# Low parts of streamed weights: VectorE's subtraction, or ScalarE's negation and an accumulating DMA

## The chip, the cores and the metric

The kernel runs on one core of a Trainium2 chip. Its engines work side by side, each on its own queue, in order, and wait for one another by semaphores: TensorE (PE; its weight loads are PEld), VectorE (DVE), ScalarE (ACT), GpSimd (POOL) and SyncE (SP, which here only starts DMAs). Sixteen DMA engines move data for all queues. The metric is device microseconds of one execution; a time is the median of several runs.

## The reference

Two decoder layers on 512 tokens of width 1024, all in float32. Layer 0 mixes tokens by gated linear attention (GLA), layer 1 by a gated DeltaNet in chunks; after each comes a ConvFFN of inner width 2816, and after every part a LayerNorm of the scaled residual:

```python
for i in range(DEPTH):                       # 2
    y = gla_mixer(h, ...) if i % 3 == 0 else gdn_mixer(h, ...)
    h = layer_norm(ALPHA * h + y, ln_g[i, 0], ln_b[i, 0])
    h = layer_norm(ALPHA * h + conv_ffn(h, ffn_w_in[i], ffn_conv_w[i], ffn_w_out[i]),
                   ln_g[i, 1], ln_b[i, 1])

def conv_ffn(x, w_in, conv_w, w_out):
    h = causal_dwconv(x @ w_in, conv_w)
    gate, up = jnp.split(h, 2, axis=-1)
    return (gelu(gate) * up) @ w_out
```

Most of the work is x @ w with large weights. The DeltaNet also solves a lower triangular system in each chunk, from which the small matmuls called V and R below come.

## The kernel before

**Three products for one.** A float32 matrix product is made from parts in the rounded type float32r: a = ah + al, w = wh + wl, and a w is taken as ah wh + ah wl + al wh. So for each weight block a high part (wh, the block rounded) and a low part (wl, the block minus wh) must be formed on the chip.

**A block's way.** All weights are streamed once, in the order of a plan (`plan_fm`, `plan_tm`, `plan_out`, `plan_pad`, `plan_rep`), in blocks of 128 x 1024 floats, 512 KB. `issue` (line 202) handles one: SP starts the load into a tile `raw` (three buffers, `RAWB`), ScalarE casts it to `wh` (line 243), VectorE subtracts to get `wl` (line 244). `wh` and `wl` have four buffers each (`WB`). In an "fm" block the eight pieces of 128 x 128 are held still in the PE array and the 512 columns of x stream past: 8 x 3 = 24 matmuls, `fm_mms`, line 286. In a "tm" block the activations are held still and two rows of 512 weight columns stream past for four token blocks: 2 x 4 x 3 = 24 matmuls as well, `tm_half`, line 342. All matmuls are issued in `mm`, line 155.

**The last blocks of a sublayer** (`TAIL` = 4) lie in ordinary activation slots (`wsh`, `wsl`, lines 233 and 234, in two halves), so that the token blocks can be finished one after another and the four large buffers already hold the next sublayer's first blocks. A sublayer that follows a LayerNorm begins with four blocks on the first half of the tokens, then the same four on the second half (`HEADSTART`), since the second half of x comes later. Each block's buffer is given back only after its second half.

**How far ahead.** `weight()` hands out the next block and calls `prefetch`, which issues blocks up to `look` ahead of those taken, as long as fewer than four large buffers are held. `look` is `LOOKAHEAD`, 2, and larger at a tail. This sets the order in which the program is written; the framework's scheduler then orders each engine's queue by its own estimate of when things are ready, except PE, whose order mostly follows the generator tasks. Those are spawned by the code and paced by an estimated PE clock (`clk`, `pump`), and `vec` adds VectorE's estimated work to it.

**What else uses POOL and SP.** Residual tiles are scaled and shifted on POOL after a LayerNorm (lines 583 and 584, sixteen operations in each of two sublayers). The DeltaNet's residual goes to DRAM and back by POOL's queue (lines 576, 606, 609). In the DeltaNet, `base` (line 1068) runs a forward substitution of 31 steps on VectorE for all chunks at once (lines 1078 and 1080), copies the result (line 1083), stores it (SP, lines 1084 and 1085) and loads it back in pieces T and rm (SP and POOL, lines 1097 and 1100); `inverse` (line 1108) builds the chunk inverses from them by the matmuls V and R.

Of the kernel before, what the change touches and what calls it, by code (L numbers as in the profile page):

```python
# [8 lines left out]
F32 = mybir.dt.float32  # L9
# [4 lines left out]
ALU = mybir.AluOpType  # L14
# [3 lines left out]
S = 512  # L18
# [13 lines left out]
SLOTS = 53  # L32
RAWB = 3
WB = 4
LOOKAHEAD = 2
TAIL = 4
HEADSTART = 4
INV_DELAY = 18.0
# [10 lines left out]
def blk(i, n=P):  # L49
    return slice(i * n, i * n + n)  # L50


class Trunk:
# [148 lines left out]
    def issue(self, item):  # L202

        nc = self.nc
        if item[0] == "rep":
            return self.issue_rep(*item[1:])
        used = 1024
        raw = self.raw if self.issued == 0 else self.rp.tile([P, 1024], F32, name=self.uid("raw"), tag="raw")
        if self.issued == 0:
            pass  # L210
        elif item[0] == "fm":
            _, w, col = item
            nc.sync.dma_start(
                raw.rearrange("p (c f) -> p c f", c=NC),
                w[:, col:col + P].rearrange("(c p) f -> p c f", p=P))
        elif item[0] == "tm":
            _, w, row, n, col, _ = item
            used = n * S
            nc.sync.dma_start(
                raw[:, :used].rearrange("p (j f) -> p j f", j=n),  # L220
                w[row:row + n * P, col:col + S].rearrange("(j p) f -> p j f", p=P))
        else:
            nc.gpsimd.memset(raw, 0.0)
            r3 = raw.rearrange("p (c f) -> p c f", c=NC)
            for w, col, n, at in item[1]:
                nc.sync.dma_start(
                    r3[:, :, at:at + n],
                    w[:, col:col + n].rearrange("(c p) f -> p c f", p=P))
        if self.in_slots(item):
            w = []  # L230
            for j in range(used // S):
                wh, wl = self.slot("wsh", F32R), self.slot("wsl", F32R)
                nc.scalar.copy(wh, raw[:, blk(j, S)])
                nc.vector.tensor_sub(wl, raw[:, blk(j, S)], wh)
                self.vec(0.7)
                w.append((wh, wl))
            return w
        self.held += 1
        wh = self.wp.tile([P, 1024], F32R, name=self.uid("wh"), tag="wh")
        wl = self.wp.tile([P, 1024], F32R, name=self.uid("wl"), tag="wl")  # L240
        for n in (S, used) if self.issued == 0 else (used,):
            cols = slice(0 if n < used or self.issued else S, n)
            nc.scalar.copy(wh[:, cols], raw[:, cols])  # L243
            nc.vector.tensor_sub(wl[:, cols], raw[:, cols], wh[:, cols])  # L244
        self.vec(1.24)
        return [(wh[:, blk(j, S)], wl[:, blk(j, S)]) for j in range(used // S)]

    def issue_rep(self, w, col):

        nc = self.nc  # L250
        raw = self.rp.tile([P, 1024], F32, name=self.uid("raw"), tag="raw")
        r3 = raw[:, :P].rearrange("p (c f) -> p c f", c=NC)
        nc.sync.dma_start(r3, w[:, col:col + 16].rearrange("(c p) f -> p c f", p=P))
        self.held += 1
        wt = self.wp.tile([P, 1024], F32R, name=self.uid("wh"), tag="wh").rearrange("p (c f) -> p c f", c=NC)
        w5 = wt[:, :, :96].rearrange("p c (r t f) -> p c r t f", r=3, t=2)
        src = r3.unsqueeze(2).to_broadcast([P, NC, 3, 16])
        nc.scalar.copy(w5[:, :, :, 0, :], src)
        nc.vector.tensor_sub(w5[:, :, :, 1, :], src, w5[:, :, :, 0, :])
        return wt  # L260
# [109 lines left out]
    def out_proj(self, a, n, first, final):  # L370
# [3 lines left out]
        for hf in range(2):  # L374
# [20 lines left out]
            self.tm_half(a, n, TAIL if last else 1, done, last)  # L395
        self.look = LOOKAHEAD

# [60 lines left out]
    def load_x(self, x):  # L458
# [34 lines left out]
        def second():  # L493
            for tb in range(2, NTB):
                self.after = self.x_parts(tb)
                yield 1.2
            self.look = LOOKAHEAD

# [869 lines left out]
```

## Time and profile before

| | us |
|---|---|
| median of 3 runs | 1295.02 |
| lowest, highest run | 1292.35, 1297.74 |
| span of the profiled execution | 1300.2 |
| TensorE, VectorE, ScalarE, GpSimd busy in it | 1279.0, 790.2, 546.8, 111.0 |

The profile is of one execution. Of it only the span, from the first to the last instruction, is known; it lies 5.2 us above the median of the timed runs. Matmuls overlap in their pipeline, so the busy time of PE hides short gaps, and the mean of one matmul (370 to 390 ns) is longer than the time from one to the next; that is read from the chain, as a stretch divided by its matmuls. Idle time of an engine is put down to what ended it, in square brackets.

### The profile page before, as it was taken

The numbers are of one execution on the slowest core, as the hardware profiler recorded it, in microseconds if no ns is written. First come the engines' busy times: TensorE is split into PE (matmuls) and PEld (weight loads), VectorE is DVE, ScalarE is ACT, GpSimd is POOL, SyncE is SP. The second block draws the span as 40 slices with busy tenths as digits, with TensorE's granted clock in tenths as the row PEclk, the third lists the DMA queues.
The fourth block names the chain that finished last, engine by engine and source line by source line (L and its number), as shares of the span: only waits on it lengthen the run. The fifth ranks groups of instructions, "written<-read, shape, count | busy, mean of one in ns | idle before, by whom it ended". The sixth has DMA issues, their size and how long they took to land.

```text
span 1300.2 us, 17238 instructions
## 1 busy us (share of the span) xinstructions
PE 1279.0 (98%) x6666; PEld 1078.1 (83%) x6666; DVE 790.2 (61%) x1442; ACT 546.8 (42%) x1030; POOL 111.0 (9%) x150
## 2 busy tenths in 40 slices
PE   8999999999999999999999999999999999999996
PEld 6878888988888888889788889988888888888885
DVE  3673366676643466655799835669677653366656
ACT  3554443634421344425865535543554431244420
POOL 4000000070000000001111310100034000000000
PEclk9999999999999999999999968999999999999999
DMA  6421224143333333251543420333143333333331
GB/s 181 117 81 49 77 86 130 33 130 114 98 97 97 97 97 98 87 143 66 135 117 106 127 49 17 115 98 113 49 137 107 97 98 98 97 97 97 97 98 65
DMA packets 167089, 126.52 MB, mean 97 GB/s; under 512 B 16088, under 2 KB 139546, under 8 KB 167008
## 3 DMA queue, kind: packets, MB, share of 16 engines
q1 hardware_dynamic: 161728, 115.10, 30.0%
q0 software_dynamic: 3888, 8.50, 2.1%
q10 hardware_dynamic: 1392, 1.84, 0.4%
q8 instruction: 52, 0.85, 0.3%
q14 instruction: 29, 0.24, 0.1%
HBM read 119.63 MB, written 5.78 MB: 96 GB/s over the span
## 4 chain that ended last, share of the span: by engine, by line
PE 86%; issue 6%; DVE 5%; DMA 1%; ACT 1%; POOL 1%; DVEq 0%; POOLq 0%; ACTq 0%
PE fm L155 45%; PE tm L155 32%; PE o L155 1%; PE V L155 1%; PE R L155 1%; PE xT L166 1%; PE vn L155 1%; DVE ln_st L386 1%; PE pg L155 1%; PE yT L166 1%; PE qkT L166 1%; PE pq L155 0%; DMA gla_nw<-in_gla_norm_w_dram 0%; DVE wl L244 0%; DVE conv L940 0%
## 5 line engine op out<-in xcount | busy, mean ns | idle before, releaser
L244 DVE TENSOR_TENSOR wl<-raw,wh 128x1024 fp32r<-128x1024 f32 (+1 forms) x190 | 238.3, 1255 | 321.1 <-ACT wh L243 319.3
L155 PE MATMUL fm<-xh,wh 128*128 128x512 f32 (+1 forms) x1104 | 408.3, 370 | 0.4 <-ACT wh L243 0.4
L155 PE MATMUL fm<-xl,wh 128*128 128x512 f32 (+1 forms) x1104 | 404.8, 367 | 0.0
L155 PE MATMUL fm<-xh,wl 128*128 128x512 f32 (+1 forms) x1096 | 401.2, 367 | 2.5 <-DVE wl L244 2.5
L243 ACT CAST wh<-raw 128x1024 fp32r<-128x1024 f32 (+1 forms) x190 | 198.8, 1047 | 269.9 <-PE tm L155 159.4
L155 PEld LDWEIGHTS fm<-xh,wl 128*128 128x128 f32 x1096 | 207.4, 190 | 36.5 <-DVE wl L244 3.1
L155 PEld LDWEIGHTS fm<-xh,wh 128*128 128x128 f32 x1104 | 209.1, 189 | 34.2 <-ACT wh L243 1.2
L155 PEld LDWEIGHTS fm<-xl,wh 128*128 128x128 f32 x1104 | 209.3, 190 | 32.7
L643 DVE SCALAR_TENSOR_TENSOR conv<-fm,ffn_cw,conv 128x511 f32<-128x511 f32 (+1 forms) x176 | 130.7, 745 | 3.0
L155 PE MATMUL tm<-wl,gh 128*128 128x512 f32 x288 | 112.0, 389 | 0.0
L155 PE MATMUL tm<-wh,gh 128*128 128x512 f32 x288 | 112.0, 389 | 0.0
L155 PE MATMUL tm<-wh,gl 128*128 128x512 f32 x288 | 112.0, 389 | 0.0
L155 PE MATMUL tm<-wh,xh 128*128 128x512 f32 x192 | 79.5, 414 | 1.0 <-ACT qk L756 1.0
L417 ACT CAST gh<-conv 128x512 fp32r<-128x512 f32 x44 | 27.3, 621 | 124.7 <-DVE conv L658 124.6
L155 PE MATMUL tm<-wh,xl 128*128 128x512 f32 x192 | 75.4, 393 | 0.0
L155 PE MATMUL tm<-wl,xh 128*128 128x512 f32 x192 | 75.1, 391 | 0.0
L653 ACT ACTIVATE conv<-conv 128x512 f32<-128x512 f32 x44 | 27.8, 633 | 95.0 <-DVE conv L643 95.0
L155 PEld LDWEIGHTS tm<-wh,gh 128*128 128x128 f32 x288 | 54.1, 188 | 11.2
L155 PEld LDWEIGHTS tm<-wh,gl 128*128 128x128 f32 x288 | 54.1, 188 | 11.2
L155 PEld LDWEIGHTS tm<-wl,gh 128*128 128x128 f32 x288 | 54.1, 188 | 11.2
L641 ACT ACTIVATE conv<-fm,ffn_cw 128x512 f32<-128x512 f32 x88 | 59.9, 681 | 0.2
L940 DVE SCALAR_TENSOR_TENSOR conv<-fm,gdn_cw,conv 128x509 f32<-128x509 f32 (+2 forms) x72 | 53.2, 742 | 4.6 <-ACT conv L938 4.1
(274 smaller groups left out, 1555.4 us busy)
## 6 DMA issues: line engine op xcount, KB each, us to landing
raw<-in_ffn_w_in_dram SPq DMA_DIRECT2D x88, 512.0 KB, 3.7
raw<-in_ffn_w_out_dram SPq DMA_DIRECT2D x44, 512.0 KB, 3.7
raw<-in_gdn_w_in_dram SPq DMA_DIRECT2D x32, 512.0 KB, 4.0
raw<-in_gla_w_in_dram SPq DMA_DIRECT2D x23, 512.0 KB, 3.5
raw<-in_gla_w_out_dram SPq DMA_DIRECT2D x8, 512.0 KB, 3.5
raw<-in_gdn_w_out_dram SPq DMA_DIRECT2D x8, 512.0 KB, 3.8
hd<-h POOLq DMA_DIRECT2D x8, 256.0 KB, 2.5
dt<-drow POOLq DMA_DIRECT2D x8, 256.0 KB, 5.6
```

The costliest lines, as they stand in the source:

```text
L155: t = self.nc.tensor.matmul(out, a, b, start=start, stop=stop)
L166: t = self.nc.tensor.transpose(out, a, self.ident[:n, :n])
L243: nc.scalar.copy(wh[:, cols], raw[:, cols])
L244: nc.vector.tensor_sub(wl[:, cols], raw[:, cols], wh[:, cols])
L386: nc.vector.bn_stats(self.st[tb][:, hf, :], h)
L417: cast = self.nc.scalar.copy(dst_h, src)
L641: nc.scalar.activation(a, ps, AF.Identity, scale=tap(2))
L643: nc.vector.scalar_tensor_tensor(a[:, d:], ps[:, :S - d], tap(2 - d), a[:, d:], ALU.mult, ALU.add)
L653: nc.scalar.activation(a, a, AF.Gelu)
L940: self.conv = nc.vector.scalar_tensor_tensor(a[:, d:], ps[:, :S - d], tap(3 - d), a[:, d:], ALU.mult, ALU.add)
```

## The change

Two things change in how a low part is made, and one in how far ahead.

- From the seventh block of the plan on, and for all blocks in slots, VectorE's subtraction is gone. ScalarE writes the negated rounded block into `wl` (it reads the raw block, multiplies by -1 and rounds as it writes), and a DMA issued from POOL adds the raw block onto it, as float32: raw - round(raw). The raw tile is free only when this DMA has landed.
- The first six blocks (`DIRECT`) are made as before; one of them is the small block of `issue_rep`, which isn't changed.
- `LOOKAHEAD` is 3.

`vec` is no longer called for the low parts, so the estimate of VectorE's load that paces some tasks is smaller.

```diff
-LOOKAHEAD = 2
+LOOKAHEAD = 3
+DIRECT = 6
...
                 nc.scalar.copy(wh, raw[:, blk(j, S)])
-                nc.vector.tensor_sub(wl, raw[:, blk(j, S)], wh)
-                self.vec(0.7)
+                self.low(wl, raw[:, blk(j, S)])
...
+        if self.issued >= DIRECT:
+            nc.scalar.copy(wh[:, :used], raw[:, :used])
+            self.low(wl[:, :used], raw[:, :used])
+            return [(wh[:, blk(j, S)], wl[:, blk(j, S)]) for j in range(used // S)]
...
+    def low(self, wl, raw):
+
+        self.nc.scalar.mul(wl, raw, -1.0)
+        self.nc.gpsimd.dma_start(wl.bitcast(F32), raw, accum_op=ALU.add)
```

The new function makes every line behind it stand 9 lower. How the queues are ordered now is shown at three places.

On POOL, in the first feed-forward layer, the residual's operations (h times and plus gb) stood in one piece behind loads of constants (rows). Before:

```order
L439 DMA rows_847<-in_ffn_conv_w_dram 44x128
L439 DMA rows_849<-in_gdn_conv_w_dram 96x128
L583 TENSOR_TENSOR h_95<-h_95,gb_2425 128x512
L583 TENSOR_TENSOR h_97<-h_97,gb_2425 128x512
L583 TENSOR_TENSOR h_96<-h_96,gb_2427 128x512
```

Now, with the accumulating DMAs (wl from raw; wl_2530 is the low part of the layer's block 11, wl_2573 of block 12):

```order
L592 TENSOR_TENSOR h_97<-h_97,gb_2494 128x512
L255 DMA wl_2530<-raw_2527 128x1024
L593 TENSOR_TENSOR h_95<-h_95,gb_2498 128x512
L592 TENSOR_TENSOR h_96<-h_96,gb_2496 128x512
L593 TENSOR_TENSOR h_97<-h_97,gb_2498 128x512
L593 TENSOR_TENSOR h_96<-h_96,gb_2500 128x512
L592 TENSOR_TENSOR h_98<-h_98,gb_2496 128x512
L592 TENSOR_TENSOR h_99<-h_99,gb_2494 128x512
L593 TENSOR_TENSOR h_98<-h_98,gb_2500 128x512
L593 TENSOR_TENSOR h_99<-h_99,gb_2498 128x512
L592 TENSOR_TENSOR h_100<-h_100,gb_2496 128x512
L592 TENSOR_TENSOR h_101<-h_101,gb_2494 128x512
```

One more operation of this kind follows, and then the DMA for wl_2573: eleven stand between the two. Three more stand ahead of block 13's. The second feed-forward layer has the same pattern.

On VectorE, at the end of the DeltaNet's substitution (tt and tmp are its steps, dt the decay matrices multiplied by PE's products pq, conv the short convolutions). Before, from the first product with pq on:

```order
L1054 TENSOR_TENSOR dt_5226<-dt_5226,pq_6114 128x512
L1080 TENSOR_TENSOR tt_4778<-tt_4778,tmp_5769 128x9x23
L1078 TENSOR_TENSOR tmp_5769<-m_798_4779,tt_4778 128x192
L1080 TENSOR_TENSOR tt_4778<-tt_4778,tmp_5769 128x8x24
L1078 TENSOR_TENSOR tmp_5769<-m_798_4779,tt_4778 128x175
L1080 TENSOR_TENSOR tt_4778<-tt_4778,tmp_5769 128x7x25
L244 TENSOR_TENSOR wl_6235<-raw_6232,wh_6234 128x1024
```

Seventeen more rows stand between these and the copy of line 1083. Now:

```order
L1063 TENSOR_TENSOR dt_5344<-dt_5344,pq_6244 128x512
L1089 TENSOR_TENSOR tt_4883<-tt_4883,tmp_5893 128x2x30
L1087 TENSOR_TENSOR tmp_5893<-m_798_4884,tt_4883 128x31
L1089 TENSOR_TENSOR tt_4883<-tt_4883,tmp_5893 128x31
L1092 COPY m_798_4884<-tt_4883 128x1024
```

The first product with pq comes at the same place among PE's matmuls; on VectorE the substitution is all but finished there.

On PE, where the inverse begins. Before, after the eighteen matmuls of a block that follow the third pq (the last two are shown):

```order
L155 MATMUL fm_6238<-xl,wh_6085 128x512
L155 MATMUL fm_6238<-xh,wl_6086 128x512
L155 MATMUL V_6285<-T_6060,am_5522 32x32 x4
L155 MATMUL V_6285<-T_6060,am_5558 32x32 x4
L155 MATMUL V_6286<-T_6060,am_5522 32x32 x4
L155 MATMUL V_6286<-T_6060,am_5558 32x32 x4
L155 MATMUL R_6311<-V_6284,rm_6062 32x32 x4
```

Now, after six matmuls of that block:

```order
L156 MATMUL fm_6370<-xl,wh_6139 128x512
L156 MATMUL fm_6370<-xh,wl_6140 128x512
L156 MATMUL V_6417<-T_6189,am_5644 32x32 x4
L156 MATMUL V_6417<-T_6189,am_5680 32x32 x4
L156 MATMUL V_6418<-T_6189,am_5644 32x32 x4
L156 MATMUL V_6418<-T_6189,am_5680 32x32 x4
L156 MATMUL fm_6370<-xh,wh_6139 128x512
```

The first V is asked for twelve matmuls earlier, and nine large matmuls now stand between V and R. On SP a load of a raw tile stands just ahead of the first load of T, before and now; it waited for a subtraction and now waits for an accumulating DMA.

## The prediction

> **What bounds the kernel now.** I read the page's head first, then the chain of work that ended last, the list of what TensorE (PE) waited for, and the windows by stage.
>
> ```profile
> span 1300.2 us, 17238 instructions
> PE 1279.0 (98%) x6666; PEld 1078.1 (83%) x6666; DVE 790.2 (61%) x1442; ACT 546.8 (42%) x1030; POOL 111.0 (9%) x150
> L244 DVE TENSOR_TENSOR wl<-raw,wh 128x1024 fp32r<-128x1024 f32 (+1 forms) x190 | 238.3, 1255 | 321.1 <-ACT wh L243 319.3
> L243 ACT CAST wh<-raw 128x1024 fp32r<-128x1024 f32 (+1 forms) x190 | 198.8, 1047 | 269.9 <-PE tm L155 159.4
> ```
>
> The work to be replaced is VectorE's largest group, but VectorE is busy 61% and PE 98%. In the chain the two feed-forward layers are unbroken matmuls:
>
> ```profile
> 367.94 65.28 PE tm L155 x288
> 433.22 108.80 PE fm L155 x480
> ```
>
> Both rows give 0.227 us a matmul. Every weight block of 512 KB feeds 24 matmuls of 512 columns, so PE takes a block every 24 x 0.227 = 5.44 us, in both row kinds. Nothing that VectorE gives up can shorten that. What it can shorten is the list of PE's waits (the five longest of those that hang on weights, VectorE or the inverse):
>
> ```profile
> PE fm L155 <- DVE wl L244: 2.5, 3, 1.3
> PE V L155 <- DMA T<-dinvt: 1.1, 2, 0.6
> PE qkT L166 <- ACT conv L942: 1.1, 2, 0.7
> PE R L155 <- DMA rm<-dinv: 0.6, 1, 0.6
> PE xT L166 <- DVE ln_rs L538: 0.6, 1, 0.6
> ```
>
> and one stretch in which TensorE's clock was not granted in full. The columns of a window are its length, then busy time by engine, granted clock, DMA share and GB/s:
>
> ```profile
> 640.00:740.00 100.00, 98.80 (x509) 82.77 (x509) 91.76 (x245) 60.59 (x145) 19.66 (x39) 1.00 0.42 121
> 740.00:800.00 60.00, 58.26 (x609) 49.96 (x608) 24.00 (x53) 21.92 (x69) 11.19 (x20) 0.74 0.20 45
> 1270.00:1300.20 30.20, 19.90 (x88) 16.15 (x86) 22.08 (x60) 0.00 (x0) 0.00 (x0) 0.92 0.19 69
> 745.00:750.00 5.00, 4.40 (x53) 4.00 (x48) 1.53 (x6) 1.93 (x9) 4.83 (x9) 0.57 0.40 67
> ```
>
> In 640 to 740 VectorE is full (91.76 of 100): it runs the DeltaNet's forward substitution among the subtractions. Then the clock falls: 60 x (1 - 0.74) = 15.6 us of full-speed work are lost. The last 10 us (30.20 - 19.90) are the final LayerNorm, which has no weights in it.
>
> **The change part by part.**
>
> *VectorE loses* 184 subtractions of 128x1024 and 32 of 128x512 (the first five whole blocks stay): 184 x 1.255 + 32 x 0.68 = 253 us, of 790.
>
> ```profile
> L233 ACT CAST wsh<-raw x32: 609/620/632, 193.2 to 1252.9; 128x512 fp32r<-128x512 f32 x32
> L234 DVE TENSOR_TENSOR wsl<-raw,wsh x32: 675/683/693, 193.9 to 1253.6; 128x512 fp32r<-128x512 f32 x32
> ```
>
> *ScalarE gains* as many multiplications by -1. The trace has none of that shape; the cast beside it reads and writes the same sizes, so 184 x 1.05 + 32 x 0.62 = 213 us, making 760 of 1300 us. It stays below PE in every window (the fullest hundred, 640 to 740, goes from 61 to about 61 + 18 x 1.05 = 80).
>
> *What VectorE's room is worth.* In the substitution it sits in the way like this:
>
> ```profile
> 727.01 0.68 DVE L1054 TENSOR_TENSOR dt<-dt,pq 128x512 f32<-128x512 f32 x1
> 736.47 1.09 DVE L1083 COPY m<-tt 128x1024 f32<-128x1024 f32 x1
> 737.47 1.22 DVE L244 TENSOR_TENSOR wl<-raw,wh 128x1024 fp32r<-128x1024 f32 x1
> ```
>
> ```profile
> 742.89 0.66 PE L155 MATMUL V<-T,am 32*32 32x32 f32 x16 [0.65 <-DMA T<-dinvt]
> 746.29 0.63 PE L155 MATMUL R<-rm,V 32*32 32x32 f32 x8 [0.60 <-DMA rm<-dinv]
> ```
>
> Before, the copy that ends the substitution comes 9.5 us after the first product with pq; in the new order only three short steps lie between them, so the copy ends about 727.0 + 0.7 + 0.6 + 1.1 = 729.4, some 8 us earlier. PE asks for T twelve matmuls (2.7 us) earlier, so some 5 us remain for the two stores, the queue and the loads: the waits on T and rm go. What is late next there is SP, on which a raw load that waits for an accumulating DMA now stands ahead of the loads of T. Of the five waits above, 5.9 us in all, I count 5 us as gone (bounds 0 and 5.9).
>
> *The clock.* Whether it falls again is not settled by the trace. Less waiting and a more even mix with large matmuls speak for a shallower dip, the same tiny 32x32 matmuls against. Bounds 0 and -15.6; I take half, -7.8, because the fall begins in the very window that holds the two waits.
>
> *The DMA engines* get 184 accumulations of 512 KB and 32 of 256 KB. Neither their length nor their load is in the trace; the nearest rows are plain copies:
>
> ```profile
> q1 hardware_dynamic: 161728, 115.10, 30.0%
> raw<-in_ffn_w_in_dram SPq DMA_DIRECT2D x88, 512.0 KB, 3.7
> dinvt<-tt SPq DMA_DIRECT2D x1, 512.0 KB, 2.7
> 650.00:655.00 5.00, 5.00 (x23) 4.11 (x23) 3.78 (x8) 2.74 (x11) 0.00 (x0) 1.00 1.02 356
> ```
>
> Queue q1: 0.300 x 1300.2 = 390 us of all sixteen engines for 115.1 MB, 1.78 us a block. The fullest window moves 356 GB/s, 1.47 us a block. An accumulation reads two blocks and writes one, so one pass (1.5) to three (5.3) bound it; I take two full passes, 2.9 us, since a plain copy also reads and writes in one pass. With the load that is 4.7 of the 5.44 us: it fits, with little room. The Trainium skill's page "Collectives: The Full Stack", section "The bandwidth ceiling: the fold count and why AG ≠ RS ≠ AR", says the add itself costs nothing and the second read halves the rate (62.28 against 32.35 GB/s); by it an estimate is 1.93 x 1.47 = 2.8 us, and the sum would stay; no row here shows an accumulation. For the time from issue to landing I take the 2.7 us of the plain 512 KB copy plus one pass, 4.2 to 4.5: 4.4 us (bounds 2.7 and three times that, 8.1).
>
> *Is that hidden?* In a feed-forward layer ScalarE starts a block when PE frees the buffer of the block four back:
>
> ```profile
> 443.91 1.05 ACT L243 CAST wh<-raw 128x1024 fp32r<-128x1024 f32 x1 [0.96 <-PE fm L155]
> 444.86 0.68 ACT L641 ACTIVATE conv<-fm,ffn_cw 128x512 f32<-128x512 f32 x1
> ```
>
> Cast, conv and negation take 2.8 us, the issue on POOL 0.54 (row below), the landing 4.4: 7.7 us, against three blocks, 16.3 us. The raw tile is held 7.7 us and reloaded in 3.7 plus 0.4 of issue: 11.8 of the same 16.3 us for three raw tiles. Hidden at up to 12.2 us for the two landings together. Cost 0; this cover, three blocks of PE work, is also what "three ahead" keeps in program order.
>
> ```profile
> L576 POOL DMA_DIRECT2D hd<-h x8: 539/540/604, 584.5 to 605.2; - x8
> 614.40 1.05 ACT L243 CAST wh<-raw 128x1024 fp32r<-128x1024 f32 x1 [4.72 <-PE fm L155]
> 617.23 1.05 ACT L243 CAST wh<-raw 128x1024 fp32r<-128x1024 f32 x1 [1.20 <-PE fm L155]
> ```
>
> *At the start of a layer* the cover is thinner: four blocks are held until their second halves are done, 2.83 us apart. The fifth block is cast at 614.40, negated by 616.5, issued by 617.0, landed by 621.4; PE wants it at 614.40 + 3 x 2.83 + 0.45 = 623.3. Cost 0, at 8.1 us of landing 1.8 us, in three layers.
>
> *POOL's queue* is in order, and now carries the weights:
>
> ```profile
> 269.34 6.03 POOL L583 TENSOR_TENSOR h<-h,gb 128x512 f32<-128x512 f32 x4 [180.96 <-DMA gb<-in_ln_g_dram]
> L583 POOL TENSOR_TENSOR h<-h,gb x16: 1284/1514/2279, 269.3 to 983.6; 128x512 f32<-128x512 f32 x16
> 250.39 1.05 ACT L243 CAST wh<-raw 128x1024 fp32r<-128x1024 f32 x1 [6.35 <-PE fm L155]
> 253.27 1.05 ACT L243 CAST wh<-raw 128x1024 fp32r<-128x1024 f32 x1 [1.24 <-PE fm L155]
> ```
>
> The new order puts eleven of its residual operations between two accumulations. Block 5 of the layer starts at 250.39 + 3 x 2.88 = 259.0 and block 12 at 259.0 + 7 x 5.44 = 297.1. Block 11 is ready for issue at 275.3 + 2.8 = 278.1; eleven operations of 1.51 us end at 295.2; block 12 is issued by 295.8 and lands at 300.2, but its low part is wanted at 297.1 + 0.45: PE waits 2.7 us. It happens in both feed-forward layers: +5.4 us. Bounds: 0.2 us each with the shortest operations (1.284), 6.4 with a landing of 8.1.
>
> *The sum:* -5 - 7.8 + 5.4 = -7.4 us. The profiled execution (span 1300.2) lies 5.2 above the timed median of 1295.0, so I apply the difference to the median: **1287.6 us**. Its bounds without the extremes together: 1275 to 1302.
>
> **The rivals.**
>
> *1. The clock dip stays and the rest cancels.* For it: the tiny matmuls are all still there. The Trainium skill's page "TensorE: Matmul & The Clock Gate", section "What's actually happening", has half clock follow an idle window of about 3.4 us; by it the 0.65 us waits would not be its cause. The trace disagrees in part, as the clock fell to 0.57 with no longer wait. Time: -5 + 5.4, 1295.
>
> *2. The DMA engines become the bound.* With the load at 1.78 us, PE is overtaken once an accumulation takes over 5.44 - 1.78 = 3.7 us of all engines. Three passes at the fastest rate are 4.4 us: 6.2 us a block, 0.75 x 184 = 138 us slower, about 1425; at q1's rate 1600. For it: no row shows an accumulation; against it: two passes fit.
>
> *3. Landings are hidden in the mean but not at the seams.* At 8.1 us the two residual places cost 6.4 each and the three layer starts 1.8 each, 18 us, and a window like that of 745 to 750 loses 2 us of clock; with the 5 us won and the dip in place, about 1295 + 18 + 2 x 2 - 5 = 1312. It decides from a landing of about 6 us. For it: POOL's waits and residual work stand ahead of weights; against it: the plain copy's 2.7 us.
>
> **How the numbers follow.** The forecast has 0.50, rival 1 0.17, rival 2 0.18, rival 3 0.15. About 0.5% (6.5 us) is what a measurement of this kernel can tell from no change: faster means below 1288.5. Of the forecast's own range (1275 to 1302) seven tenths lie there, and a fifth of rival 1: 0.35 + 0.03 = 0.38. Slower: rivals 2 and 3 and a little of the forecast, 0.35. Same: 0.27. The range 1274 to 1335 takes in the forecast, rivals 1 and 3 and the mildest of rival 2, and leaves out most of rival 2.
>
> **What would show it.** Right: VectorE near 537 us, ScalarE near 760; in 370 to 540 PE still at 0.227 us a matmul with no waits; landings of 4 to 5 us; a DMA share near 0.8; the granted clock of the inverse's stretch well above 0.74; short waits on wl where POOL does the residual. Wrong: matmuls in the feed-forward layers spaced by waits on wl or wh (rival 2); a dip as deep as before (rival 1); waits on wl at all five seams (rival 3).

## The result, and the profile after

The changed kernel takes **1353.54 us** (median of 4 runs, 1346.74 to 1354.32) against 1296.38 for the kernel before beside it (1292.35 to 1303.21): a ratio of 1.0418, 95% interval 1.0375 to 1.046. It is slower by 57 us; the prediction had 1287.6, a range up to 1335, and faster as the likeliest sign. One of the ten runs of gdn_only, below, took 3290.79 us and is left out of its ratio.

The page of the changed kernel, in the rows that answer those of before:

```profile
span 1351.4 us, 17750 instructions
PE 1289.6 (95%) x6666; PEld 1079.9 (80%) x6666; DVE 559.6 (41%) x1226; ACT 733.0 (54%) x1246; POOL 288.2 (21%) x366
q0 software_dynamic: 34992, 113.37, 45.9%
wl<-raw POOLq DMA_DIRECT2D x184, 512.0 KB, 5.7
L255 POOL DMA_DIRECT2D wl<-raw x184 | 158.9, 867 | 871.1 <-ACT wl L254 796.9
```

VectorE lost 231 us of work, ScalarE gained 186, and no engine is fuller than PE. POOL's software queue q0 now moves 113 MB; the median accumulation lands 5.7 us after its issue, and the issue takes 0.87 us of POOL. The steady stretch of the feed-forward layers, where most of the blocks are, lost nothing. First the chain of work, then the window over the same stretch (length, busy time by engine, clock, DMA share, GB/s):

```profile
383.71 65.28 PE tm L156 x288
448.99 108.59 PE fm L156 x479
```

```profile
383.00:557.00 174.00, 174.00 (x770) 144.06 (x769) 49.32 (x68) 88.23 (x104) 27.59 (x32) 1.00 0.89 194
```

PE is busy for 174.00 of 174 us at full clock with the DMA engines 0.89 busy, at the same 0.227 us a matmul as before. From 1060 to 1255, in the second of these layers, it is busy throughout as well. So the 51 us by which the span grew lie elsewhere. What PE waited for longest (total, times, longest):

```profile
PE fm L156 <- DMA wl<-raw: 16.2, 2, 8.7
PE xT L167 <- ACT h L560: 12.2, 3, 4.6
PE qkT L167 <- ACT conv L951: 6.5, 3, 5.1
PE tm L156 <- DMA wsl<-raw: 5.6, 6, 2.3
PE fm L156 <- DVE wl L248: 2.4, 3, 1.3
```

These sum to 43 us and name the places, but not how much each cost. That is read by lining up the two traces: PE runs as many matmuls in both, so the start of the matmul with the same number of matmuls ahead of it, after less before, is the delay at that point; where it grows, time is lost. (The first chain row: 383.71 - 367.94 = 15.8 us late.) The table has the growth in each stretch of the time of before, in us, for all kernels of this study:

| kernel | tail 1 (215 to 262) | residual 1 (to 310) | tail 2 (575 to 625) | DeltaNet (to 735) | inverse (to 800) | tail 3 (895 to 945) | residual 2 (to 1010) | tail 4 (1255 to 1288) | elsewhere | span less 1300.2 |
|---|---|---|---|---|---|---|---|---|---|---|
| after | 6.1 | 10.2 | 7.1 | 12.3 | -10.8 | 11.0 | 11.1 | 5.1 | -0.9 | 51.2 |
| load_only | 0.3 | 0.0 | 0.0 | 2.8 | -0.8 | 6.0 | 0.0 | 0.0 | 4.3 | 12.6 |
| no_load | -0.3 | 0.0 | 0.0 | 0.7 | 5.7 | 4.0 | 0.0 | 0.0 | 4.8 | 14.9 |
| raw4 | -0.3 | 7.6 | 6.5 | 3.1 | -10.2 | 5.5 | 8.2 | 0.0 | -0.5 | 19.9 |
| resid_dve | 7.8 | 1.3 | 10.3 | 6.9 | -11.4 | 13.1 | 3.2 | 6.0 | 0.3 | 37.5 |
| raw4_resid | -0.3 | 0.0 | 7.2 | 4.3 | -10.6 | 9.6 | 0.0 | 0.0 | -0.4 | 9.8 |
| tails_sub | -0.3 | 14.1 | 0.1 | 4.1 | -3.1 | 3.9 | 14.0 | 0.0 | -1.0 | 31.8 |
| before_raw4 | 0.0 | 0.0 | 0.0 | 0.0 | -1.6 | -0.8 | 0.0 | 0.0 | 0.0 | -2.4 |
| look3 | -0.3 | 0.0 | 0.0 | 0.7 | 1.8 | -0.7 | 0.0 | 0.0 | -0.5 | 1.0 |
| gdn_only | -0.3 | 0.0 | 0.1 | 6.3 | -11.7 | 5.6 | 0.0 | 0.0 | 1.6 | 1.6 |
| gdn_look2 | 0.0 | 0.0 | 0.1 | 7.7 | -11.3 | 3.4 | 0.0 | 0.0 | -0.1 | -0.2 |
| gdn_late | 0.0 | 0.0 | 0.0 | 0.6 | -10.4 | 4.7 | 0.0 | 0.0 | 2.1 | -3.0 |
| inv26 | 0.0 | 0.0 | 0.0 | 0.0 | -13.2 | 0.2 | 0.0 | 0.0 | -0.2 | -13.2 |

A profile is one execution, and some executions lie off their median: those of gdn_look2, load_only and raw4 some 6 us below it, that of no_load 7 above. That of the kernel before lies some 5 above: a time is 1.7 us longer than its span wherever both are known, so its span of 1300.2 stands for some 1301.9 us against 1296.38. That is why the spans differ by 51 us and the medians by 57. The table says where; how much in all is said by the ratios.

In the changed kernel 29 us go at the four ends of sublayers, 21 at the two places where POOL does the residual, 12 in the DeltaNet ahead of the inverse, and 11 come back in the inverse.

**A residual place.** POOL's timeline in the first feed-forward layer (start, length, instruction, idle before it and what ended that):

```profile
282.46 0.85 POOL L255 DMA_DIRECT2D wl<-raw  x1 [5.02 <-ACT wl L254]
287.83 2.54 POOL L592 TENSOR_TENSOR h<-h,gb 128x512 f32<-128x512 f32 x2 [4.52 <-DMA gb<-in_ln_g_dram]
290.32 0.86 POOL L255 DMA_DIRECT2D wl<-raw  x1
291.79 1.53 POOL L593 TENSOR_TENSOR h<-h,gb 128x512 f32<-128x512 f32 x1 [0.60 <-DMA gb<-in_ln_b_dram]
...
304.93 1.28 POOL L593 TENSOR_TENSOR h<-h,gb 128x512 f32<-128x512 f32 x1
306.13 0.86 POOL L255 DMA_DIRECT2D wl<-raw  x1
```

The eleven operations are there as foreseen, but they end at 306.1: POOL stood idle for gb, which used to be there at 269.34. The queue of SP shows why, before and after:

```profile
263.86 1.05 SPq L520 DMA_DIRECT2D gb<-in_ln_g_dram  x2
264.95 0.91 SPq L520 DMA_DIRECT2D gb<-in_ln_b_dram  x2
```

```profile
262.78 19.27 SPq L214 DMA_DIRECT2D raw<-in_ffn_w_in_dram  x5
282.14 1.01 SPq L529 DMA_DIRECT2D gb<-in_ln_g_dram  x2
283.20 0.91 SPq L529 DMA_DIRECT2D gb<-in_ln_b_dram  x2
```

gb is issued 18.3 us later on a PE that is 5.5 us late: 12.8 us too late. Ahead of it in SP's queue stand loads of raw tiles, which here wait for accumulations to land; whether these waits made it late is taken up with no_load below. Behind PE's wait on wl the granted clock was low as well:

```profile
310.00:315.00 5.00, 4.28 (x10) 3.41 (x11) 0.06 (x1) 0.00 (x0) 2.89 (x3) 0.50 0.61 152
```

**A tail.** ScalarE at the end of the first sublayer, before and after. The first row is its last cast (before) or its last long wait (after) in the burst of eight blocks issued there, the last row the LayerNorm's first activation:

```profile
210.40 1.06 ACT L243 CAST wh<-raw 128x1024 fp32r<-128x1024 f32 x1 [4.29 <-PE tm L155]
219.45 0.82 ACT L551 ACTIVATE h<-h,ln_nb,ln_rs 128x512 f32<-128x512 f32 x1 [8.00 <-DVE ln_nb L550]
```

```profile
222.50 1.04 ACT L242 CAST wh<-raw 128x1024 fp32r<-128x1024 f32 x1 [9.60 <-DMA raw<-in_ffn_w_in_dram]
...
225.35 1.05 ACT L254 ACTIVATE wl<-raw 128x1024 fp32r<-128x1024 f32 x1
226.30 0.80 ACT L560 ACTIVATE h<-h,ln_nb,ln_rs 128x512 f32<-128x512 f32 x1
```

Before, ScalarE was 8 us early for the LayerNorm; now it sits 9.6 us in front of an empty raw tile with the LayerNorm behind it in its queue, and is 6.9 us late. The stretch lost 6.1.

**The DeltaNet.** VectorE, where the substitution begins, before and after:

```profile
694.92 0.18 DVE L1078 TENSOR_TENSOR tmp<-m,tt 128x31 f32<-128x31 f32 x1
```

```profile
729.72 0.19 DVE L1087 TENSOR_TENSOR tmp<-m,tt 128x31 f32<-128x31 f32 x1 [11.38 <-DMA m<-dblk]
```

VectorE has the room it was meant to get, and spends 11.4 us of it waiting for the blocks of am to go to DRAM and back, with the convolutions queued behind; PE's 5.1 us on conv follow. Before, it went from other work straight into this step. The step comes 34.8 us later on a PE that is 27.5 us late, so 7.3 us too late.

### The profile page after: what moved, and what is told of

The parts are those of the page before. It is cut to its first block, busy times and chain, and to the rows that moved or that the text cites. A ratio compares the mean times of both kernels' runs of the same rounds, so it can differ in the third digit from the quotient of the medians.

```text
span 1351.4 us, 17750 instructions
## 1 busy us (share of the span) xinstructions
PE 1289.6 (95%) x6666; PEld 1079.9 (80%) x6666; DVE 559.6 (41%) x1226; ACT 733.0 (54%) x1246; POOL 288.2 (21%) x366
## 3 DMA queue, kind: packets, MB, share of 16 engines
q0 software_dynamic: 34992, 113.37, 45.9%
## 4 chain that ended last, share of the span: by engine, by line
PE 59%; DMA 19%; issue 9%; DVE 6%; ACT 4%; POOL 3%; SPq 1%; POOLq 0%; DVEq 0%; ACTq 0%
PE fm L156 32%; PE tm L156 20%; DMA wl<-raw 5%; DMA raw<-in_ffn_w_in_dram 2%; DMA raw<-in_ffn_w_out_dram 2%; DMA gb<-in_ln_b_dram 2%; DMA raw<-in_gdn_w_in_dram 2%; DMA wsl<-raw 2%; DVE conv L949 1%; PE o L156 1%; DMA raw<-in_gla_w_in_dram 1%; POOL h L593 1%; POOL h L592 1%; DVE tmp L1087 1%; ACT wh L242 1%
## 5 line engine op out<-in xcount | busy, mean ns | idle before, releaser
L156 PE MATMUL fm<-xh,wl 128*128 128x512 f32 (+1 forms) x1096 | 401.8, 368 | 18.6 <-DMA wl<-raw 16.2
L255 POOL DMA_DIRECT2D wl<-raw x184 | 158.9, 867 | 871.1 <-ACT wl L254 796.9
L242 ACT CAST wh<-raw 128x1024 fp32r<-128x1024 f32 x184 | 191.9, 1043 | 178.2 <-DMA raw<-in_ffn_w_in_dram 80.0
L254 ACT ACTIVATE wl<-raw 128x1024 fp32r<-128x1024 f32 x184 | 193.9, 1054 | 115.7 <-PE tm L156 108.4
L388 DVE SCALAR_TENSOR_TENSOR h<-h,tm 128x512 f32<-128x512 f32 x32 | 21.9, 686 | 141.7 <-PE tm L156 141.7
L949 DVE SCALAR_TENSOR_TENSOR conv<-fm,gdn_cw,conv 128x511 f32<-128x511 f32 (+2 forms) x72 | 53.3, 744 | 24.8 <-ACT conv L947 23.9
L156 PEld LDWEIGHTS tm<-wh,gh 128*128 128x128 f32 x288 | 54.1, 188 | 11.3
L156 PEld LDWEIGHTS tm<-wh,gl 128*128 128x128 f32 x288 | 54.1, 188 | 11.3
L156 PEld LDWEIGHTS tm<-wl,gh 128*128 128x128 f32 x288 | 54.1, 188 | 11.1
```

Of the source, the lines that this page charges most:

```text
L156: t = self.nc.tensor.matmul(out, a, b, start=start, stop=stop)
L242: nc.scalar.copy(wh[:, :used], raw[:, :used])
L254: self.nc.scalar.mul(wl, raw, -1.0)
L255: self.nc.gpsimd.dma_start(wl.bitcast(F32), raw, accum_op=ALU.add)
L388: nc.vector.scalar_tensor_tensor(h, h, ALPHA, ps, ALU.mult, ALU.add)
L949: self.conv = nc.vector.scalar_tensor_tensor(a[:, d:], ps[:, :S - d], tap(3 - d), a[:, d:], ALU.mult, ALU.add)
```

## The experiments

Theory A: the time is lost in chains and in-order queues, because a raw tile is held longer and because weights now stand in POOL's queue. Theory B: it is the load on the DMA engines, which makes every transfer late.

**load_only and no_load: the load without the dependence.** Subtraction on VectorE; the DMAs go to scratch tiles, or are left out. Both have four activation slots fewer, to make room for the scratch tiles.

```diff
-        self.nc.scalar.mul(wl, raw, -1.0)
-        self.nc.gpsimd.dma_start(wl.bitcast(F32), raw, accum_op=ALU.add)
+        self.nc.vector.tensor_sub(wl, raw, wh)
+        self.dump ^= 1                      # these three lines in load_only alone
+        n = wl.shape[1]
+        self.nc.gpsimd.dma_start(self.dumps[self.dump][:, :n], wh.bitcast(F32), accum_op=ALU.add)
```

> VectorE makes every low part again; the same number of accumulating DMAs of the same sizes is still issued from POOL, but each adds a finished high part onto one of two scratch tiles that nothing reads (four activation slots fewer make the room). So the DMA engines carry the whole load, no weight waits for it, and a raw tile is free after the subtraction. Theory A (the time is lost in chains and in-order queues: weights queued behind POOL's residual, raw tiles held until a landing, ScalarE's LayerNorm behind casts that wait for such tiles): 1296 to 1306 us, no waits on wl of more than 3 us at the residual places, delay against before at the four tails together under 8 us instead of 29. Theory B (the load itself: transfers of weights, gb, T and the decay blocks come late because sixteen engines are 0.9 busy): 1335 us or more, with the same late loads of gb and m.

> The kernel of load_only without its accumulating DMAs: VectorE's subtraction everywhere, three blocks ahead, four slots fewer, the pacing as in the changed kernel. It is the control for load_only, which ended 12.6 us after the kernel before in its profile. If the load of the DMA engines alone costs little (theory A), most of the 12.6 us remain or go with POOL's queue: 1296 to 1312 us. If the load explains all of it: equal to the kernel before, 1293 to 1299 us. Three ahead without any DMA should not be worth over 3 us either way.

load_only: 1320.67 us, ratio 1.0176 (1.0128 to 1.0223). no_load: 1309.48, ratio 1.0101 (1.0067 to 1.0136). The load of load_only, in its page:

```profile
q0 software_dynamic: 34992, 113.37, 50.0%
```

It carries as many packets and bytes as the changed kernel, at a greater share, and yet loses nothing at the residual places and 6.3 us at the tails instead of 29. Theory B falls as the main cause: the load alone is worth 11 us by the two medians, 10 by the two ratios, of 57. The other 13 are in no_load too, which hardly differs from the kernel before but in its pacing, its three blocks ahead and its slots; look3, below, has 0.5% of it by three ahead alone, and the rest wasn't parted. load_only lies between the ranges of the two theories. Theory A's number, 1306 at most, was too low, for it left both out.

no_load also corrects the reading of gb above. There too gb is issued late, although no load waits for a landing:

```profile
276.92 1.05 SPq L532 DMA_DIRECT2D gb<-in_ln_g_dram  x2
```

PE is 4.3 us late there, so gb comes 8.7 us too late, and nothing is lost, because no weight stands behind POOL's operations. So the order of SP's queue can make most of the 12.8 us without any accumulation; what makes a late gb cost is the accumulating DMAs behind POOL's operations.

**raw4 and before_raw4: a fourth raw tile.**

```diff
-SLOTS = 53
-RAWB = 3
+SLOTS = 51
+RAWB = 4
```

> The changed kernel with four raw tiles instead of three (two activation slots fewer make the room). Theory A: at a tail the burst of eight blocks is paced by raw tiles that are held until their accumulation lands, so a fourth takes away a quarter of the round trip: the four tails lose about 12 us instead of 29, the residual places stay unless gb comes earlier behind the shorter queue of SP: 1325 to 1340 us. Theory B: as many bytes through the same engines, 1350 to 1356 us.

> The kernel before with four raw tiles and two slots fewer, the control for raw4. Before, a subtraction frees a raw tile some 3 us after its load, so a fourth tile should do nothing where PE never waits: 1292 to 1298 us. If four tiles gained the 31 us of raw4's span over the changed kernel by something other than the longer hold, a part of it would show here: 1285 us or less.

raw4: 1327.6 us, ratio 1.0259 (1.0198 to 1.032): 26 us less than the changed kernel by the medians, 21 by the ratios, 31 by the two profiles. before_raw4: 1299.2, ratio 0.9997 (0.9973 to 1.0021). Not a byte less is moved, and about half of the loss is gone: tails 1 and 4 wholly, tail 3 by half, the DeltaNet from 12.3 to 3.1. ScalarE at tail 1 in raw4:

```profile
212.05 1.05 ACT L242 CAST wh<-raw 128x1024 fp32r<-128x1024 f32 x1 [10.09 <-DMA raw<-in_ffn_w_in_dram]
...
219.64 0.82 ACT L560 ACTIVATE h<-h,ln_nb,ln_rs 128x512 f32<-128x512 f32 x1
```

It still waits long for a tile, but ten us earlier, and the LayerNorm starts within 0.2 us of where it did before. The kernel before does nothing with a fourth tile, so it is the longer hold that needs it. Tail 2 hardly moved (7.1 to 6.5). In its burst, in raw4 too, all sixteen DMA engines are full:

```profile
570.00:580.00 10.00, 10.00 (x46) 8.27 (x45) 5.36 (x8) 4.10 (x8) 2.29 (x3) 1.00 1.09 274
580.00:590.00 10.00, 10.00 (x46) 8.28 (x45) 2.50 (x9) 3.96 (x5) 3.73 (x5) 1.00 1.10 201
```

There a further tile would have little to win, and the load works together with the hold; load_only has shares of 1.06 and 1.07 in this burst and loses nothing, as nothing in it waits for a landing. But tail 1 has a share of 1.11 in raw4 and did gain, so this stays open.

**resid_dve and raw4_resid: the residual off POOL**, with three and with four raw tiles.

```diff
-            nc.gpsimd.tensor_mul(h[hf], h[hf], gb[hf])
-            nc.gpsimd.tensor_add(h[hf], h[hf], gb[2 + hf])
+            nc.vector.tensor_mul(h[hf], h[hf], gb[hf])
+            nc.vector.tensor_add(h[hf], h[hf], gb[2 + hf])
```

> The changed kernel with the residual's thirty-two operations on VectorE instead of POOL, so that no accumulating DMA stands behind them. Theory A: the two waits on wl of 8 us and the slow clock behind each go, 10 + 11 us: about 1333 us. If the late gb now stalls VectorE's queue instead, a part of it comes back there: up to 1350. Theory B: the landings are late at these places too, so little moves: 1345 to 1355 us.

> The changed kernel with both mends: four raw tiles and the residual on VectorE. If the two places of loss are separate (theory A), their gains add: of the 19.9 us by which raw4 ends later than the kernel before, 15.8 are its residual places, of which resid_dve kept 4.4: some 8.5 us late, a median of 1302 to 1310. If both mends only relieve the same shared load (theory B), they do not add: 1320 to 1328.

resid_dve: 1339.74 us, ratio 1.0338 (1.0292 to 1.0383); raw4_resid: 1312.18, ratio 1.0121 (1.008 to 1.0161). What PE waits for on wl in resid_dve, and the longest of PE's waits in raw4_resid:

```profile
PE fm L156 <- DMA wl<-raw: 3.5, 3, 1.3
```

```profile
PE xT L167 <- ACT h L560: 7.5, 2, 3.9
PE tm L156 <- DMA wsl<-raw: 4.4, 4, 3.6
PE fm L156 <- DVE wl L248: 2.0, 2, 1.3
```

The residual places shrink from 21 to 4.5 us, and to nothing with four tiles; some 8 us come back at the tails in resid_dve, for a reason that no run shows (tail 1, ahead of both places, already loses 1.7 more). The two mends add: 26 us for the tile, then 15 more by the medians, where the residual alone gave 14, as separate causes would. raw4_resid ends 2 us above the range that was expected.

**tails_sub: no accumulating DMA in the bursts.**

```diff
-                self.low(wl, raw[:, blk(j, S)])
+                nc.vector.tensor_sub(wl, raw[:, blk(j, S)], wh)
+                self.vec(0.7)
...
-        if self.issued >= DIRECT:
+        if self.issued >= DIRECT and self.look <= LOOKAHEAD:
```

> The changed kernel with VectorE's subtraction for all blocks issued in the bursts at the ends of sublayers (the halves in slots and the four blocks of the next sublayer), accumulating DMAs for all the others. Theory A: the 6 + 7 + 11 + 5 = 29 us of the four tails go, the two residual places (21 us) and the DeltaNet stay: 1322 to 1330 us. Theory B: the load falls in the bursts alone, the rest stays late; raw and gb still land late there: 1335 to 1350 us.

1331.55 us, ratio 1.0264 (1.0215 to 1.0314), 1.5 us above theory A's range. The tails go from 29 to 3.7 us. This takes the hold and the load of the bursts away together, so it shows that the accumulating DMAs there are the cause, and not by which of the two. The residual places grow from 21 to 28: PE waits for landings of wl four times instead of twice, 19.2 us in all instead of 16.2. That the late gb and the operations hit harder once the tails are on time fits this, and isn't tested.

**gdn_only, gdn_look2, gdn_late and look3: what the change is good for.** gdn_only is tails_sub with accumulating DMAs in the DeltaNet alone (the edit below is against tails_sub). gdn_look2 is gdn_only with two blocks ahead, gdn_late is gdn_look2 with accumulating DMAs from the DeltaNet's thirteenth block on. look3 is the kernel before with three blocks ahead and nothing else.

```diff
-        if self.issued >= DIRECT and self.look <= LOOKAHEAD:
+        if self.accum[0] <= self.issued < self.accum[1] and self.look <= LOOKAHEAD:
...
+    lo = len(t.plan)
     t.gdn_plan(gdn_w_in[0], gdn_w_out[0])
+    t.accum = lo, len(t.plan)               # gdn_late: lo + 12
```

> Accumulating DMAs only for the DeltaNet's blocks that are not issued in a burst; VectorE's subtraction for all others. Three blocks ahead, three raw tiles. The runs so far lose nothing steady in the DeltaNet but up to 12 us before the inverse, and win 3 to 11 us of clock in it. If the clock's gain comes from VectorE's room in the substitution: 1286 to 1293 us. If the gain is only the other side of the waits that go ahead of it (tails_sub had 4 us of them and won 3 back): 1294 to 1300 us. No waits on wl in the feed-forward layers in either case.

> gdn_only with weights two ahead, as before the change. If gdn_only's losses at its start (1.9 us) and at the DeltaNet's tail (5.6 us) come from three ahead: 7.5 us less than gdn_only, 1294 to 1299 us, no slower than the kernel before, with the 11.7 us of the inverse kept and 5 us still lost ahead of it. If they come from something else: like gdn_only, 1301 to 1306 us.

> gdn_look2 with accumulating DMAs from the DeltaNet's thirteenth block on only; the first twelve, while the gates and decays are made, are subtracted. If the 4.9 us that gdn_only lost there come from transfers and ScalarE work among the short steps of the gates: 1289 to 1294 us, faster than both kernels. If they are lost to anything that stays (waits just before the substitution): 1294 to 1299 us.

> The kernel before with weights three ahead, nothing else. If the lookahead is worth nothing while PE never waits for a block: 1294 to 1300 us. If it brings loads and subtractions forward into the DeltaNet's tail, where no_load and gdn_only both lost 4 to 6 us ahead of the LayerNorm: 1300 to 1305 us, with a wait of xT on VectorE there.

Ratios: gdn_only 1.0048 (1.0029 to 1.0067), gdn_look2 1.0068 (1.0042 to 1.0093), gdn_late 0.9985 (0.9967 to 1.0002), look3 1.005 (1.0027 to 1.0073). All three DeltaNet kernels win 10 to 12 us in the inverse, where the clock stays up. The window of 740 to 800 in gdn_look2, gdn_late and look3:

```profile
740.00:800.00 60.00, 57.70 (x673) 50.12 (x672) 25.98 (x61) 30.07 (x87) 17.13 (x29) 0.97 0.51 114
```

```profile
740.00:800.00 60.00, 58.38 (x681) 50.73 (x680) 25.87 (x66) 30.23 (x96) 12.65 (x21) 0.94 0.43 94
```

```profile
740.00:800.00 60.00, 54.58 (x599) 47.41 (x598) 22.81 (x49) 20.41 (x66) 10.57 (x19) 0.77 0.21 55
```

The waits on T of gdn_look2 and of look3:

```profile
PE V L156 <- DMA T<-dinvt: 2.3, 1, 2.3
```

```profile
PE V L155 <- DMA T<-dinvt: 5.4, 2, 3.1
```

Several expectations failed. gdn_only, at 1304.07 us, lies above both of its ranges: the inverse's gain came, and was spent elsewhere. gdn_look2, at 1307.49, does so too; two ahead did not mend gdn_only, so that theory of its losses falls. look3, at 1303.86, is as slow as its second case had it, but not where it said: its waits on T grew to 5.4 us, and tail 3 lost nothing. gdn_late, at 1296.74, did lose only 0.6 us ahead of the inverse instead of 7.7, so the first twelve blocks, among the gates' short steps, are the costly ones. Its gain was eaten at tail 3, 4.7 us, by a wait that no run explains. It doesn't need an accumulation: no_load has it with 3.4 us. The row of gdn_late:

```profile
PE xT L167 <- DVE ln_rs L548: 3.8, 1, 3.8
```

**inv26: a later start of the inverse.** The kernel before, with the inverses' tasks started later. Between the first V and R PE now has six large matmuls, and six more ahead of the next V; before, V, R, the products qkT and pq and the next V followed one another without any.

```diff
-INV_DELAY = 18.0
+INV_DELAY = 26.0
```

> The kernel before with another start time of the inverses' tasks (INV_DELAY 26 instead of 18), so that six large matmuls stand between the first V and R, and six more before the next V, much as in the changed kernel, while VectorE still subtracts. If the new order of PE alone kept the clock up: 1285 to 1291 us and a clock above 0.9 in the inverse. If it takes VectorE's room as well: 1293 to 1300 us and a clock near 0.75.

1287.73 us (1285.92 to 1288.7), ratio **0.9918** (0.9895 to 0.994): faster than both kernels, in one number and without any accumulating DMA. The same window:

```profile
740.00:800.00 60.00, 59.53 (x699) 51.82 (x698) 34.89 (x73) 29.38 (x101) 13.17 (x22) 1.00 0.29 77
```

The clock is 1.00 where it was 0.74, so VectorE's room isn't needed for that. The later start changes two things at once: the order, and PE's waits on T and rm, which are gone. Waits alone don't bring the dip: gdn_look2 waits for T for 2.3 us in one piece, longer than any wait of the kernel before there (0.65), and keeps 0.97. Nor is the order alone sure to lift it: around the first V the changed kernel, raw4 and tails_sub have their matmuls in exactly the same order, and tails_sub's profile dips all the same (0.80 from 758 to 818 too):

```profile
740.00:800.00 60.00, 58.15 (x596) 48.82 (x597) 27.04 (x61) 28.70 (x75) 18.22 (x32) 0.80 0.52 123
```

The granted clock of whole runs was 0.984 to 0.994 in the kernel before beside inv26 (20 runs, 1293.22 to 1304.66 us) and 0.996 to 0.998 in inv26 (6 runs, 1285.92 to 1288.7 us).

## Why the prediction was wrong, point by point

- **VectorE and ScalarE.** Right: 560 us (forecast 537) and 733 (760).
- **Steady feed-forward layers at no cost.** Right: 0.0 us lost in 310 to 575, at a DMA share of 0.89. The two landings took 5.7 us (accumulation) and 5.3 us (the load of `ffn_w_in`) in the median, 11.0 of the 12.2 us of room that the prediction gave them (12.6 by its own terms), so little was left.
- **An accumulation as two passes, 2.9 us.** Right: q0 went from 2.1% to 45.9%; 0.459 x 1351.4 less 0.021 x 1300.2 is 593 us of all engines, for 184 whole and 32 half blocks 2.96 us a block. The Trainium skill's page "Collectives: The Full Stack", section "The bandwidth ceiling: the fold count and why AG ≠ RS ≠ AR", gave an estimate of 2.8, by a halved rate that it states for rings of cores; the trace agrees, with 2.96. Rival 2, at 4.4 us and more, is out.
- **Landing 4.4 us, issue 0.54.** Too small: 5.7 and 0.87. The bounds held the first; the second had only the plain copy's row.
- **Layer starts and tails at no cost.** This step failed, by 29 us. I sized the start of a layer by the *fifth* block, whose cover is thin, and took the eight blocks of the burst before it as given. They go through three raw tiles, each held from its load until its accumulation lands, and the LayerNorm stands behind them on ScalarE. I had worked out that round trip (11.8 of 16.3 us) in the steady state alone. tails_sub shows that the accumulating DMAs of the bursts cost this time, and raw4 that at tails 1 and 4, and for half of tail 3, it is the hold of the raw tiles. At tail 2 the hold alone isn't shown to be the cause.
- **Residual places at 2.7 us each.** Right place, wrong size: 10.2 and 11.1. The eleven operations did stand between two accumulations, but I took their start from the trace of before. gb came 12.8 us too late, through SP's queue (in no_load 8.7, with no accumulation at all). I named SP's queue for the loads of T and did not follow it to gb. resid_dve and raw4_resid show that the loss hangs on POOL's operations: 4.5 us and nothing. Of the first wait, 2.7 us are the queue as worked out, 5.4 the later end of the operations (306.1 - 5.5 - 295.2); the later landing and the slow clock behind the wait (0.50 in 310 to 315) would make up the rest.
- **Five us of waits won.** Wrong. The 2.5 us on VectorE's wl lie at the first blocks, which the change leaves alone (2.4 after). The wait on rm did go; that on T stayed (1.1 before, 1.2 after), and that on conv grew from 1.1 to 6.5. In all the DeltaNet ahead of the inverse lost 12.3 us, which the sum had at nothing: the substitution began 7.3 us too late, behind the transfers of am.
- **Half the clock dip regained, -7.8.** The right size: the inverse's stretch won 10.8. The window that answers 740 to 800:

```profile
775.00:825.00 50.00, 49.03 (x616) 42.73 (x617) 18.61 (x48) 24.88 (x72) 12.29 (x20) 0.93 0.42 92
```

  My reason, the two waits in it, is not what decides: gdn_look2 waits 2.3 us on T and gdn_late 1.6, and their clocks are 0.97 and 0.94. inv26 shows that a later start of the inverse, with large matmuls between the small ones, lifts it; tails_sub shows that the order is not all. The Trainium skill's page "TensorE: Matmul & The Clock Gate", section "What's actually happening", ties the half clock to how busy PE was in a window of about 3.4 us. Behind the first residual place's wait on wl, 7.5 us, the trace agrees (0.50 in 310 to 315). At the dip no run here has a pause of that length; that tiny matmuls in a row count as little work is argued from inv26, not shown by it.
- **Rival 3 was nearest**: landings hidden in the mean but not at the seams. Its point of decision (landings of about 6 us) was met, its price, 18 us of seams, was about a third of what came. It priced each landing by itself, where the cost came from queues in which one late landing holds up all that stands behind.

So the sum was -5 - 7.8 + 5.4, and the profile has: waits ahead of the inverse +12, the inverse -11, residual places +21, tails +29.

**What stays open:** why tail 2 did not gain from the fourth tile; what the rest of no_load's 13 us is; the wait of 3 to 4 us at tail 3 in no_load and in the kernels with accumulations in the DeltaNet; and why the clock dipped in tails_sub (-3.1 us in the inverse) with the same order of PE there that raw4 has (-10.2). The changed kernel with inv26's delay was not tried.

## What to carry to other kernels

When a step moves from a compute engine to a DMA, don't compare its latency with the steady state alone: follow the buffer that is now held until the landing, and every in-order queue in which something waits for that buffer, at each seam where many blocks are issued at once. A steady state can be unharmed at 0.9 of the DMA engines' time while the seams lose four per cent. And when a stretch at a low clock is to be won back, try when its small matmuls start, and what stands between them, before moving work between engines.

## What the runs showed of the hardware

- An accumulating DMA from SBUF to SBUF took 2.96 us of all sixteen engines for 512 KB, landed 5.7 us after its issue in the median (4.5 to 9.8), and its issue kept POOL for 0.87 us, against 0.54 for plain copies from the same queue.
- At a DMA share of 0.89 over 174 us PE lost nothing.
- The granted clock of a stretch of tiny matmuls went from 0.74 to 1.00 when they started later, with large ones between them and without waits; with the dip the spread of the runs went too, from 11.4 us (20 runs) to 2.8 (6 runs). The same order of matmuls had 0.93 in the profile of the changed kernel and 0.80 in that of tails_sub.
